# Seven block products for eight in the widening product of a decoder MLP (fp32 split in two halves), one core

## The chip, the core and the metric

One core of a Trainium2 chip runs the whole program. The metric is device time in microseconds (us), the median over runs. Engines: TensorE (PE; PEld is its weight load), VectorE (DVE), ScalarE (ACT), GpSimd (POOL), SyncE (SP, which issues most DMAs). Each engine works through its own queue in order.

## The reference, cut to what matters

Two layers over 576 tokens (512 of a prompt and 64 of a sample), model width 1024, MLP width 4096. Only the MLP at the end of a layer is touched by the change:

```python
    x = x + mixed @ w_o
    h2 = rmsnorm(x, norm2)
    x = x + jnp.square(jax.nn.relu(h2 @ w_up)) @ w_down
```

## The kernel before

Activations lie with features on the partitions: a tile of 128 features x 576 tokens. Every fp32 operand of a large product is cut into a high part (rounded to fp32r by a ScalarE cast) and a low part (what is left, by a VectorE subtraction). A product of two such operands is three matmuls: high x high, high x low, low x high. `gemm` (L222) makes one output tile: 8 k-tiles x 3 x 2 token ranges (256 and 320 columns, `HALF`), 48 matmuls, in one of two PSUM tiles (`mm`, two banks each).

Weights come as a list `seq` of 128 x 1024 tiles. `wfetch` (L106) issues their DMA on SP into `raw` (two slots), `wsplit` (L114) puts the ScalarE cast into `wh` (three slots) and notes the VectorE subtraction into `wl`, `settle` (L128) issues the noted subtractions. `wnext` (L132) is called where a weight tile is first used: there the cast of the tile two places ahead is put into ScalarE's queue, and its subtraction follows 1.2 us later by the planner's clock. The cast cannot run before TensorE has finished with the tile one place back, whose slot it takes.

The order of all queues is written by a planner: `tick` (L160) adds the estimated time of matmuls just issued to a clock `now`, and runs every generator in `sides` whose due time has come; a generator yields the delay to its next step. `post` puts a function there, `until` ticks until an event is due.

Around the change, in the layer loop:

- The product with w_o: eight output tiles f. `pair8` (L239) makes the first two, interleaved. Each is added to the residual `xs[f]` (VectorE), multiplied by the gain and split into `h2[f]`, then squared on ScalarE; GpSimd adds the squares into `sqs` (VectorE for f = 7).
- `stats` (L283), due 2.4 us after the last of these by the planner: TensorE sums `sqs` over features (`st`), VectorE and ScalarE form the reciprocal root (`rs`, with a ScalarE Sqrt), five VectorE products (`dg`), and TensorE spreads the result (`rps`) which ScalarE copies to `rb`.
- The widening product: chunks c of eight output tiles. For each, `gemm8` and then the generator `relu2`: VectorE takes max with 0 times `rb` (`z`), ScalarE squares (`zz`) and casts, VectorE subtracts, and one step of `movers` follows: a VectorE 1x1 copy (`beat`), a GpSimd 1x1 copy (`pace`) and a GpSimd DMA of a piece of the cache (`out_s`).
- The narrowing product `down` of chunk c - 1 follows the widening product of chunk c; in the last layer `last` takes the place of the last `down`.

Of the kernel before, what the change touches and what calls it, by code (L numbers as in the profile page):

```python
# [31 lines left out]
NCONST = _n  # L32

UNITS = ("d", "a", "b", "e", "c")


@with_exitstack
def hybrid_decoder_kernel(ctx: ExitStack, tc: tile.TileContext, a, o):
# [36 lines left out]
    def g2(l, k):  # L75
        return gains[:, 16 + 8 * l + k:16 + 8 * l + k + 1]
# [10 lines left out]
    for l in range(L):  # L87
        for p in range(2):
            for u, unit in enumerate(UNITS):
                if unit == "e" and p == 1:  # L90
                    continue
                seq += [(a["wq"][l, p, u, i], 1024) for i in range(2)]
        seq += [(a["wu"][l, g], 1024) for g in (3, 2, 1, 0)]
        for wg, wp_, m, lead in (("wgb", "wpb", 512, LEADB), ("wga", "wpa", 256, LEADA)):
            for f in range(8):
                seq += [(a[wg][l, i], 1024) for i in range(lead[f - 1] if f else 0, lead[f])]
                seq.append((a[wp_][l, f], m))
        seq += [(a["wo"][l, f], 1024) for f in range(8)]
        for c in range(5):
            if c < 4:  # L100
                seq += [(a["wup"][l, 8 * c + f], 1024) for f in range(8)]
            if c:
                seq += [(a["wd"][l, c - 1, f], 1024) for f in range(8)]
    raws, cut, owed, spare = [], [], [], []
    pos = [0, 0, 0]

    def wfetch(n):
        while pos[0] < min(n, len(seq)):
            src, w = seq[pos[0]]
            raw = wp.tile([128, 1024], F32, tag="raw", name="raw", bufs=2)  # L110
            Q.dma_start(raw[:, :w], src)
            raws.append((raw, w))
            pos[0] += 1

    def wsplit(n):
        while pos[1] < min(n, len(seq)):
            raw, w = raws[pos[1]]
            if pos[1] < len(seq) - 5:
                hi = wp.tile([128, 1024], F32R, tag="wh", name="wh", bufs=3)
                lo = wp.tile([128, 1024], F32R, tag="wl", name="wl", bufs=3)  # L120
            else:
                hi, lo = (spare.pop(0)().rearrange("p i n -> p (i n)") for _ in range(2))
            S.copy(hi[:, :w], raw[:, :w])
            owed.append((lo[:, :w], raw[:, :w], hi[:, :w].bitcast(F32)))
            cut.append((hi, lo))
            pos[1] += 1

    def settle():  # L128
        while owed:
            V.tensor_sub(*owed.pop(0))  # L130

    def wnext():  # L132
        i = pos[2]
# [102 lines left out]
    def gemm8(w, acts):  # L236
        return gemm([(*wcols(w, k), acts[k]) for k in range(8)])

    def pair8(acts):  # L239
        ws = wnext(), cut[pos[2]]  # L240
        tiles = [mmp.tile([128, 1024], F32, tag="mm", name="mm") for _ in range(2)]
        for n, ks in ((0, range(7)), (1, range(4)), (0, range(7, 8)), (1, range(4, 8))):
            for k in ks:
                for j, (m, x) in enumerate(((0, 0), (0, 1), (1, 0))):
                    for t0, t1, c0 in HALF:
                        T.matmul(tiles[n][:, c0:c0 + t1 - t0], wcols(ws[n], k)[m], acts[k][:, x, t0:t1],  # L246
                                 start=(k == 0 and j == 0), stop=(k == 7 and j == 2))
                tick(0.72)
        return [ps[:, 256:832] for ps in tiles]
# [106 lines left out]
    for l in range(L):  # L356
# [667 lines left out]
        for f in range(8):  # L1024
            pg = gates(LEADA, f)
            if f == 0:
                until("D", 1)
                dec_stack.close()
                mp_ = ms.enter_context(tc.tile_pool(name=f"mix{l}", bufs=8, side="right"))
            wa = wnext()  # L1030
            if pg is not None:
                gated(pg)
            ps = gemm([(*wcols(wa, k), oa[k]) for k in range(2)])
            t = gate.pop(0)
            V.scalar_tensor_tensor(out=t, in0=t, scalar=1.0, in1=ps, op0=ALU.add, op1=ALU.mult)
            (V if f == 7 else G).tensor_add(t, t, mB[f])
            m = mp_.tile([128, 2, NT], F32R, tag="m", name="m")
            split(m, t, 0.5)
            mixed.append(m)
# [5 lines left out]
        for k in range(NK):  # L1045
            xs.append(fp.tile([128, NT], F32, tag="x", name="xr"))
            post(2.1 + 0.8 * k, lambda k=k: Q.dma_start(xs[k], a["x"][k] if l == 0 else x_dr[k]))
        h2 = []
        sqs = tp.tile([128, NT], F32, tag="sqs", name="sqs", bufs=1)
        for f in range(8):  # L1050
            if f == 0:
                first = pair8(mixed)
            elif f == 1:
                wnext()
            ps = first.pop(0) if f < 2 else gemm8(wnext(), mixed)
            V.tensor_add(xs[f], xs[f], ps)
            t = fp.tile([128, 2, NT], F32R, tag="h2", name="h2")
            split(t, xs[f], g2(l, f))
            square(xs[f], sqs, f)
            h2.append(t)  # L1060
        side(stats(sqs, False, ("b", l)), 2.4)
        mark("ffn", l, lat=8.0)
        movers.append(copies(l))
        move(None)
        if l + 1 < L:
            sqs = tp.tile([128, NT], F32, tag="sqs", name="sqs", bufs=1)
        hn = []

        def down(c, fts):
            for f in range(8):  # L1070
                ps = gemm8(wnext(), fts)
                V.tensor_add(xs[f], xs[f], ps)
                if c == 3:
                    square(xs[f], sqs, f)
                    t = ap.tile([128, 2, NT], F32R, tag="a", name="a")
                    split(t, xs[f], g1(l + 1, f))
                    hn.append(t)
                    Q.dma_start(x_dr[f], xs[f])
                move(xs[f][0:1, 0:1])

        def relu2(c, ps, fts):
            t = fp.tile([128, NT], F32, tag="z", name="z", bufs=3)
            V.scalar_tensor_tensor(out=t, in0=ps, scalar=0.0, in1=scale_of["b", l][1], op0=ALU.max, op1=ALU.mult)
            t2 = fp.tile([128, NT], F32, tag="zz", name="zz", bufs=3)
            S.activation(t2, t, AF.Square)
            if c % 2 == 0:
                ft = ap.tile([128, 2, NT], F32R, tag="a", name="a")
            else:
                ft = mp_.tile([128, 2, NT], F32R, tag="m", name="m")
            split(ft, t2)  # L1090
            fts.append(ft)
            move(ft[0:1, 0, 0:1].bitcast(F32))
            return
            yield

        pend = None
        for c in range(4):
            fts = []
            for f in range(8):
                if f == 2:  # L1100
                    until("R", ("b", l))
                ps = gemm8(wnext(), h2)
                side(relu2(c, ps, fts), ("R", ("b", l)))
                tick()
            if pend is not None:
                down(c - 1, pend)
            pend = fts

        def finish(t0, t1, parts, end):
            n = t1 - t0  # L1110
# [32 lines left out]
                    yield 0.9  # L1143

        def last(fts):
            ws = []
            for t0, t1 in ((0, 320), (320, NT)):
                n = t1 - t0
                sq = tp.tile([128, NT], F32, tag="sqs", name="sqs", bufs=1)
                for f in range(8):  # L1150
                    if t0 == 0:
                        ws.append(wnext())
                    ps = mmp.tile([128, 1024], F32, tag="mm", name="mm")
                    for k in range(8):
                        for j, (w, x) in enumerate(((0, 0), (0, 1), (1, 0))):
                            T.matmul(ps[:, 0:n], wcols(ws[f], k)[w], fts[k][:, x, t0:t1],  # L1156
                                     start=(k == 0 and j == 0), stop=(k == 7 and j == 2))
                        tick(0.72 * n / NT)
                    x = xs[f][:, t0:t1]
                    V.tensor_add(x, x, ps[:, 0:n])  # L1160
                    t = sq if f == 0 else tp.tile([128, NT], F32, tag="t", name="sq")
                    S.activation(t[:, 0:n], x, AF.Square)
                    if 0 < f < 7:
                        G.tensor_add(sq[:, 0:n], sq[:, 0:n], t[:, 0:n])
                    S.activation(x, x, AF.Copy, scale=gf(f))
                    move(xs[f][0:1, t0:t0 + 1])
                side(finish(t0, t1, (sq, t), t0 > 0), 2.4 if t0 == 0 else 0.0)
            while sides:
                tick(0.3)

        if l + 1 < L:
            down(3, pend)
        else:
            spare += 8 * [lambda: fp.tile([128, 2, NT], F32R, tag="h2", name="h2")]
            spare += 2 * [lambda: ap.tile([128, 2, NT], F32R, tag="a", name="a")]
            last(pend)
        while movers:
            move(xs[7][0:1, 0:1])
        h = hn
# [127 lines left out]
```

## Time and profile before

| | us |
|---|---|
| median of three runs | 1769.35 (1768.34 to 1778.38) |
| the profiled execution | 1771.32 |
| its span, first to last instruction | 1769.3 |
| PE busy in the span | 1678.0 (95%) |
| DVE, ACT, POOL busy | 941.1, 553.6, 440.1 |
| mean granted TensorE clock | 0.971 |

A row of the groups view reads: line, engine, operation, out<-in by the program's tile names, shape, count | busy us, mean ns of one | idle time of the engine before them and who ended it. A row of the timeline reads: start us, duration us, engine, line, operation, tiles, shape, count [idle before <- who ended it]. L203 is the helper through which all VectorE, ScalarE and GpSimd operations go.

### The profile page before, as it was taken

What the parts mean: (1) busy time and instruction counts of PE and PEld (TensorE: products, weight loads), DVE (VectorE), ACT (ScalarE), POOL (GpSimd) and SP (SyncE); (2) the same over time, 40 slices, a digit from 0 to 9 for tenths busy, and PEclk for the clock granted to TensorE, in tenths of its full rate; (3) what the DMA queues carried; (4) which work ended last, traced back from release to release, by engine and by line L of the source; (5) the groups of instructions that cost most, each with busy time, mean ns of one, the idle gap of its engine ahead of it and who ended that gap; (6) DMA issues with size and microseconds to landing.
All of it is one profiled execution on the core that took longest, in us unless ns stands there. A gap on an engine that the chain in (4) does not pass through costs nothing. (4 is left out here: it accounts for less than half of the span.)

```text
span 1769.3 us, 30870 instructions
## 1 busy us (share of the span) xinstructions
PE 1678.0 (95%) x12992; PEld 1632.7 (92%) x12992; DVE 941.1 (53%) x1365; ACT 553.6 (31%) x882; POOL 440.1 (25%) x461
## 2 busy tenths in 40 slices
PE   8978799999999999999997897989999999999996
PEld 7978789989999999999997886888999999999996
DVE  6488679735444333343536975894454443433332
ACT  5523332223333222231334242311334331313232
POOL 2074129211111211110103712562111112121211
PEclk9979899999999999999999998999999999999998
DMA  5552654434254445443327336435243454444421
GB/s 171 170 163 66 219 158 127 135 105 155 85 186 165 171 155 178 153 170 109 130 74 229 118 116 208 136 100 163 78 157 120 169 168 166 167 166 164 165 84 54
DMA packets 140003, 255.22 MB, mean 144 GB/s; under 512 B 9660, under 2 KB 100284, under 8 KB 137034
## 3 DMA queue, kind: packets, MB, share of 16 engines
q1 hardware_dynamic: 135498, 198.46, 35.0%
q0 software_dynamic: 3648, 53.98, 8.6%
q8 instruction: 102, 1.67, 0.4%
q10 hardware_dynamic: 720, 0.82, 0.1%
q14 instruction: 35, 0.29, 0.1%
HBM read 239.40 MB, written 74.87 MB: 178 GB/s over the span
## 5 line engine op out<-in xcount | busy, mean ns | idle before, releaser
L228 PE MATMUL mm<-a,wh 128*128 128x256 f32 (+1 forms) x2304 | 413.2, 302 | 8.8 <-DVE tb L203 8.8
L203 DVE TENSOR_TENSOR wl<-raw,wh 128x1024 fp32r<-128x1024 f32 (+2 forms) x248 | 330.6, 1334 | 110.1 <-ACT wh L203 100.3
L203 ACT CAST wh<-raw 128x1024 fp32r<-128x1024 f32 (+2 forms) x248 | 241.4, 973 | 399.9 <-PE mm L228 301.4
L228 PEld LDWEIGHTS mm<-a,wh 128*128 128x128 f32 x2304 | 350.1, 192 | 16.9 <-issue 16.0
L228 PE MATMUL mm<-h,wh 128*128 128x256 f32 (+1 forms) x2048 | 354.8, 295 | 0.0
L228 PEld LDWEIGHTS mm<-h,wh 128*128 128x128 f32 x2048 | 306.2, 188 | 0.2
L203 POOL TENSOR_TENSOR prod<-kc,qb 128x1024 f32<-128x1024 f32 (+1 forms) x96 | 210.0, 2217 | 226.6 <-DMA kc<-in_c 183.8
L228 PE MATMUL mm<-a,wl 128*128 128x256 f32 (+1 forms) x1152 | 249.9, 299 | 0.0
L458 PE MATMUL mmq<-wh,a 128*128 128x256 f32 x1152 | 225.1, 295 | 3.2 <-DVE a L203 3.0
L228 PE MATMUL mm<-h,wl 128*128 128x256 f32 (+1 forms) x1024 | 218.1, 295 | 0.0
L203 POOL COPY pace<-beat 1x1 f32<-1x1 f32 x112 | 66.9, 597 | 545.1 <-DVE beat L203 545.1
L228 PE MATMUL mm<-m,wh 128*128 128x256 f32 (+1 forms) x1152 | 200.1, 295 | 0.0
L228 PEld LDWEIGHTS mm<-a,wl 128*128 128x128 f32 x1152 | 197.3, 192 | 0.0
L458 PEld LDWEIGHTS mmq<-wh,a 128*128 128x128 f32 x1152 | 187.4, 199 | 6.9 <-DVE a L203 3.8
L203 DVE TENSOR_TENSOR xr<-xr,mm 128x576 f32<-128x576 f32 (+2 forms) x88 | 61.5, 699 | 245.3 <-PE mm L228 223.1
L228 PEld LDWEIGHTS mm<-m,wh 128*128 128x128 f32 x1152 | 173.3, 187 | 0.0
L228 PEld LDWEIGHTS mm<-h,wl 128*128 128x128 f32 x1024 | 171.5, 188 | 0.0
L458 PE MATMUL mmq<-wl,a 128*128 128x256 f32 x576 | 167.4, 291 | 0.0
L203 ACT ACTIVATE zz<-z 128x576 f32<-128x576 f32 x64 | 43.9, 686 | 259.7 <-DVE z L203 259.7
L228 PE MATMUL mm<-m,wl 128*128 128x256 f32 x576 | 123.3, 295 | 0.0
L203 DVE SCALAR_TENSOR_TENSOR z<-mm,rb 128x576 f32<-128x576 f32 x64 | 48.5, 757 | 134.6 <-PE mm L228 128.1
L458 PEld LDWEIGHTS mmq<-wl,a 128*128 128x128 f32 x576 | 114.6, 199 | 0.0
(211 smaller groups left out, 1928.2 us busy)
## 6 DMA issues: line engine op xcount, KB each, us to landing
raw<-in_wup SPq DMA_DIRECT2D x64, 512.0 KB
raw<-in_wd SPq DMA_DIRECT2D x64, 512.0 KB
out_s<-in_c POOLq DMA_DIRECT2D x64, 508.0 KB, 4.0
kc<-in_c SPq DMA_DIRECT2D x40, 512.0 KB
raw<-in_wq SPq DMA_DIRECT2D x35, 512.0 KB
kc<-in_c SPq DMA_DIRECT2D x64, 256.0 KB
out_s<-in_c POOLq DMA_DIRECT2D x32, 504.0 KB, 4.7
raw<-in_wgb SPq DMA_DIRECT2D x16, 512.0 KB
```

The lines of the kernel that those rows point to most:

```text
L203: return op(*args, **kw)
L228: T.matmul(ps[:, c0:c0 + t1 - t0], w, act[:, x, t0:t1], start=(i == 0 and j == 0), stop=(i == n - 1 and j == 2))
L458: T.matmul(psm[:, j], x, ww, start=(k == 0 and i == 0 and j % 2 == 0), stop=(k == 7 and i == 2 and j % 2 == 1), skip_group_check=True)
```

## The change

One level of a seven-product (Strassen) scheme for h2 @ w_up. The tokens are cut in two halves of 288 (`NH`), the 1024 input features in two halves of four k-tiles, and two output tiles form a pair j (16 pairs). A pair takes seven products of four k-tiles x 3 matmuls of 288 columns, 84 matmuls in all, in place of 96 matmuls of 256 and 320 columns.

- Activations: `blocks(f)` replaces the split of `h2[f]` in the w_o stage and makes the operands B11, T1 (from f < 4) and B21, B22, T3, T2, T4 (from f >= 4 with xs[f - 4]), each split in high and low by `operand`.
- Weights: class `Two` fetches both tiles of a pair (`raw`, `raw1`). GpSimd forms two combinations in `first` (into `ws`) and, after the subtraction of the first weight tile, two in `second` (into r0 itself). A pair has four entries in the weight list, of 1024, 1024, 1024 and 512 columns, in place of two of 1024.
- `up(j)`: the product A accumulates through B11, T2, T3, T4 in one PSUM bank; ScalarE copies it out after B11 (`e1`) and T2 (`u2`) while it still grows, and after T4. T1 and B22 go to a bank `pc` (one slot) with a ScalarE copy `e5` between, B21 to a third. Three VectorE additions join them into the two tiles `z`, and `relu2` works on these.
- Chunks are of 5, 4, 4 and 3 pairs (`UPS`), each followed by the `down` of the same chunk. The last `down` and `last` begin with six k-tiles of two output tiles (`LATE`). `mp_` gets ten slots.

```diff
+    def first(self, eng):
+        h0, h1 = slice(0, 512), slice(512, 1024)
+        eng.tensor_add(self.s[:, h1], self.r1[:, h0], self.r1[:, h1])
+        eng.tensor_sub(self.s[:, h0], self.s[:, h1], self.r0[:, h0])
+
+    def second(self, eng):
+        h0, h1 = slice(0, 512), slice(512, 1024)
+        eng.tensor_sub(self.r0[:, h0], self.r1[:, h0], self.r0[:, h0])
+        eng.tensor_sub(self.r0[:, h1], self.r0[:, h1], self.s[:, h0])
...
+            two, w = seq[pos[1]]
+            then = None
+            if not isinstance(two, Two):
+                raw, w = raws[pos[1]]
+            elif w == 0:
+                raw, w = two.r0, 1024
+                two.s = fp.tile([128, 1024], F32, tag="ws", name="ws", bufs=2)
+                two.first(G)
+                then = two.second
+            else:
+                raw, w = ((two.s, 1024), (two.r0, 1024), (two.r1[:, 512:1024], 512))[w - 1]
...
         while owed:
-            V.tensor_sub(*owed.pop(0))
+            then, *args = owed.pop(0)
+            V.tensor_sub(*args)
+            if then is not None:
+                then(G)
...
+        def operand(pool, tag, bufs, src, names):
+            n = len(names)
+            t = pool.tile([128, 2, n * NH], F32R, tag=tag, name="h2", bufs=bufs)
+            S.copy(t[:, 0], src)
+            V.tensor_sub(t[:, 1], src, t[:, 0].bitcast(F32))
+            for i, name in enumerate(names):
+                ops[name].append(t[:, :, NH * i:NH * i + NH])
+
+        def blocks(f):
+            x = fp.tile([128, NT], F32, tag="z", name="z", bufs=3)
+            if f < 4:
+                S.activation(x[:, :NH], xs[f][:, :NH], AF.Copy, scale=g2(l, f))
+                V.scalar_tensor_tensor(out=x[:, NH:], in0=xs[f][:, NH:], scalar=g2(l, f), in1=x[:, :NH],
+                                       op0=ALU.mult, op1=ALU.subtract)
+                operand(ap, "a", 10, x, ("B11", "T1"))
+                return
+            S.activation(x, xs[f], AF.Copy, scale=g2(l, f))
+            operand(ap, "a", 10, x, ("B21", "B22"))
+            t = fp.tile([128, 3 * NH], F32, tag="e", name="e", bufs=1)
+            k = f - 4
+            V.scalar_tensor_tensor(out=t[:, :NH], in0=xs[k][:, NH:], scalar=g2(l, k), in1=x[:, NH:],
+                                   op0=ALU.mult, op1=ALU.subtract)
+            V.scalar_tensor_tensor(out=t[:, NH:NT], in0=xs[k][:, :NH], scalar=g2(l, k), in1=t[:, :NH],
+                                   op0=ALU.mult, op1=ALU.subtract)
+            V.tensor_sub(t[:, NT:], x[:, :NH], t[:, NH:NT])
+            operand(*((ap, "a", 10) if k < 2 else (fp, "h3", 2)), t[:, :NT], ("T3", "T2"))
+            operand(fp, "h4", 4, t[:, NT:], ("T4",))
...
-            t = fp.tile([128, 2, NT], F32R, tag="h2", name="h2")
-            split(t, xs[f], g2(l, f))
+            blocks(f)
             square(xs[f], sqs, f)
...
+        def relu2(z):
+            V.scalar_tensor_tensor(out=z, in0=z, scalar=0.0, in1=scale_of["b", l][1], op0=ALU.max, op1=ALU.mult)
+            yield 0.8
+            S.activation(z, z, AF.Square)
+            ft = mp_.tile([128, 2, NT], F32R, tag="m", name="m")
+            S.copy(ft[:, 0], z)
+            yield 1.5
+            V.tensor_sub(ft[:, 1], z, ft[:, 0].bitcast(F32))
             fts.append(ft)
             move(ft[0:1, 0, 0:1].bitcast(F32))
...
+            w = wnext()
+            product(A, w, 0, "B11", True, False)
+            S.copy(e1, A)
+            if j == 0:
+                w1 = wnext()
+                product(C_, w1, 1, "T1", True, False)
+                S.copy(e5, C_)
+            product(B, w, 1, "B21", True, True)
+            z_open()
+            V.tensor_add(z[0][:, :NH], e1, B)
+            if j:
+                w1 = wnext()
+            product(A, w1, 0, "T2", False, False)
+            S.copy(u2, A)
+            if j:
+                product(C_, w1, 1, "T1", True, False)
+                S.copy(e5, C_)
+            w = wnext()
+            product(A, w, 0, "T3", False, False)
+            z_open()
+            V.tensor_add(z[1][:, NH:], e5, A)
+            product(C_, w, 1, "B22", False, True)
+            V.tensor_add(z[0][:, NH:], u2, C_)
+            side(relu2(z[0]), ("R", ("b", l)))
+            w = wnext()
+            product(A, w, 0, "T4", False, True)
+            S.copy(z[1][:, :NH], A)
+            side(relu2(z[1]), ("R", ("b", l)))
+            tick()
```

## Rows read from the trace of the kernel before

**Rows 1.** The page: busy time of each engine over the span.
```profile
PE 1678.0 (95%) x12992; PEld 1632.7 (92%) x12992; DVE 941.1 (53%) x1365; ACT 553.6 (31%) x882; POOL 440.1 (25%) x461
```

**Rows 2.** Windows: a stretch of the second MLP (us; busy PE PEld DVE ACT POOL; PEclk; DMA; GB/s).
```profile
1400.00:1690.00 290.00, 290.00 (x2185) 290.00 (x2184) 112.32 (x163) 78.42 (x94) 49.71 (x96) 1.00 0.47 162
```

**Rows 3.** Timeline of VectorE: outputs of the widening product, second layer.
```profile
1354.62 0.76 DVE L203 SCALAR_TENSOR_TENSOR z<-mm,rb 128x576 f32<-128x576 f32 x1 [1.22 <-PE mm L228]
...
1360.97 0.76 DVE L203 SCALAR_TENSOR_TENSOR z<-mm,rb 128x576 f32<-128x576 f32 x1 [1.95 <-PE mm L228]
```

**Rows 4.** Timeline of VectorE in `last`: outputs of 24 matmuls of 320, then 256 columns.
```profile
1723.47 0.49 DVE L203 TENSOR_TENSOR xr<-xr,mm 128x320 f32<-128x320 f32 x1 [2.04 <-PE mm L1156]
1726.99 0.49 DVE L203 TENSOR_TENSOR xr<-xr,mm 128x320 f32<-128x320 f32 x1 [3.03 <-PE mm L1156]
...
1743.38 0.42 DVE L203 TENSOR_TENSOR xr<-xr,mm 128x256 f32<-128x256 f32 x1 [1.50 <-PE mm L1156]
1746.10 0.42 DVE L203 TENSOR_TENSOR xr<-xr,mm 128x256 f32<-128x256 f32 x1 [2.30 <-PE mm L1156]
```

**Rows 5.** Groups by form, 1360 to 1690 us: the MLP's VectorE and ScalarE operations.
```profile
L203 DVE TENSOR_TENSOR wl<-raw,wh 128x1024 fp32r<-128x1024 f32 x52 | 64.3, 1237 | 4.4 <-ACT wh L203 0.2
L203 ACT CAST wh<-raw 128x1024 fp32r<-128x1024 f32 x52 | 54.5, 1048 | 110.6 <-PE mm L228 110.6
...
L203 ACT ACTIVATE zz<-z 128x576 f32<-128x576 f32 x30 | 20.6, 686 | 125.0 <-DVE z L203 125.0
...
L203 DVE TENSOR_TENSOR m<-zz,m 128x576 fp32r<-128x576 f32 x16 | 12.1, 758 | 23.3 <-ACT m L203 23.3
L203 ACT CAST m<-zz 128x576 fp32r<-128x576 f32 x16 | 10.8, 673 | 0.5
```

**Rows 6.** Groups by form, whole span: GpSimd's 512-column operation and ScalarE's cast.
```profile
L203 POOL TENSOR_TENSOR prod<-kc,qb 128x512 f32<-128x512 f32 x32 | 41.5, 1318 | 22.9 <-DVE SC L203 12.3 <-DMA kc<-in_c 10.6
...
L203 ACT CAST wh<-raw 128x512 fp32r<-128x512 f32 x18 | 11.1, 615 | 39.5 <-PE mm L228 25.3 <-DMA raw<-in_wpb 12.1 <-DMA raw<-in_wq 2.1
```

**Rows 7.** Timeline: a ScalarE copy out of PSUM, near the end.
```profile
1756.21 0.37 ACT L203 COPY rb<-fb 128x256 f32<-128x256 f32 x1 [2.25 <-PE fb L1128]
```

**Rows 8.** Timeline, product with w_o: a VectorE subtraction issued during a GpSimd addition.
```profile
1315.69 1.44 POOL L203 TENSOR_TENSOR sqs<-sqs,sq 128x576 f32<-128x576 f32 x1 [4.96 <-ACT sq L203]
...
1316.52 1.69 DVE L203 TENSOR_TENSOR wl<-raw,wh 128x1024 fp32r<-128x1024 f32 x1 [0.69 <-ACT wh L203]
```

**Rows 9.** Timeline: VectorE additions from PSUM during a GpSimd addition.
```profile
1735.06 0.74 POOL L203 TENSOR_TENSOR sqs<-sqs,sq 128x256 f32<-128x256 f32 x1 [9.52 <-ACT sq L203]
...
1735.23 1.28 DVE L203 TENSOR_TENSOR xr<-xr,fb 128x320 f32<-128x320 f32 x3 [0.75 <-PE fb L1128]
```

**Rows 10.** Timeline: VectorE and ScalarE at the last w_o tile and the statistics.
```profile
1339.01 0.75 DVE L203 TENSOR_TENSOR xr<-xr,mm 128x576 f32<-128x576 f32 x1 [1.60 <-PE mm L228]
1340.61 0.82 DVE L203 SCALAR_TENSOR_TENSOR h<-xr,gains,h 128x576 fp32r<-128x576 f32 x1 [0.85 <-ACT h L203]
...
1339.80 0.78 ACT L203 ACTIVATE h<-xr,gains 128x576 fp32r<-128x576 f32 x1 [4.11 <-DVE xr L203]
...
1342.11 1.28 ACT L203 ACT_TABLE_LOAD   x1
...
1344.93 1.03 DVE L203 TENSOR_SCALAR dg<-const,rs 128x128 f32<-128x128 f32 x5
```

**Rows 11.** The chain of work that ended last, around the statistics (start, us, what).
```profile
1342.15 1.05 PE st L287 x8
...
1347.58 0.89 PE rps L308 x8
```

**Rows 12.** Windows around a TensorE stop of 8.9 us in the second layer's attention.
```profile
1070.00:1078.00 8.00, 0.00 (x0) 0.00 (x0) 1.70 (x5) 1.19 (x2) 0.88 (x5) 0.74 0.91 313
1078.00:1086.00 8.00, 6.29 (x26) 6.02 (x27) 5.05 (x14) 0.22 (x1) 6.05 (x10) 0.50 0.25 77
```

**Rows 13.** DMA issues: a cache piece, KB each, median us to landing.
```profile
out_s<-in_c POOLq DMA_DIRECT2D x64, 508.0 KB, 4.0
```

## What the change will do to the time

> **What bounds the kernel now.** I read the page first: PE is busy for 95% of the span, DVE for 53% [rows 1]. Then the windows of the MLP: TensorE has no gap in 290 us and full clock, DVE is busy for 39%, ACT for 27%, POOL for 17% [rows 2]. In this stage every matmul saved is time saved, as long as the other engines keep up. So the question is whether they do once a pair of outputs needs fewer matmuls and more of everything else. For that I read the timelines of the single engines for durations, hand-over times and for what two engines do to each other.
>
> **What is removed.** Outputs of the widening product follow each other by 6.35 us [rows 3], 48 matmuls; a pair takes 12.70. Alone, 24 matmuls of 320 columns take 3.52 us and of 256 columns 2.72 [rows 4], 0.147 and 0.113 each; halfway, a matmul of 288 is an estimated 0.131. A product of 12 is then 1.57, seven are 11.0. If TensorE stayed the bound, 32 pairs would give back 32 x 1.7 = 54 us.
>
> The Trainium skill (TensorE: Matmul & The Clock Gate, Back-to-back issue gap) gives N / 2.4 + 2.5 ns, 122.5 ns for 288 columns. By it 256 and 320 would be 109 and 136; the trace has 113 and 147 and decides. By the page's figure the sum below would be some 10 us lower (24 matmuls in each of 24 cycles, 84 in the other pairs).
>
> **What is added to a pair, by engine.** ACT: casts of 3 x 1024 and 512 columns for two of 1024, and four copies of 288 out of PSUM, estimated at 0.40 from 0.37 for 256 [rows 7]. DVE: subtractions likewise (1.24 for 1024, 0.70 estimated for 512), three additions from PSUM of 0.45 (0.42 and 0.49 for 256 and 320, [rows 4]). POOL: four operations of 512 columns, 1.3 each [rows 6]; before, only the mover's copy and DMA issue. Sums: ACT 7.9, DVE 9.2, POOL 5.2 and movers, against 11.0 of TensorE. None is over, but they are chained, and two of them meet at a port.
>
> **VectorE and GpSimd exclude each other.** In the w_o stage GpSimd adds from 1315.69 to 1317.13. A VectorE subtraction of 1024 columns that is issued at 1316.52 takes 1.69 instead of 1.24 and ends at 1318.21, 1.08 after GpSimd: about its streaming time alone [rows 8, 5]. So a VectorE operation with two SBUF inputs waits until GpSimd's operation is over. VectorE additions with one input in PSUM are not held: three of 320 columns, the first of them begun in the middle of a GpSimd addition, take 1.28 together, less than three times 0.49 [rows 9, 4].
>
> **The steady pair.** I walk the queues from the end of T1 (t = 0). Hand-overs: 0.04 from one engine to another (1339.76 to 1339.80 in [rows 10]); from the start of TensorE's next product to a reader of the last one's bank 0.2, an estimate, since a matmul's end lies behind the next one's start.
> ACT copies e5 to 0.60, casts the next pair's first weights to 1.60; DVE subtracts to 2.87. That stands ahead of the addition that frees bank A (T3 ended at 1.57, addition to 3.28), so T4 starts at 3.38, 0.24 late. GpSimd's `second` starts at 2.93: first half to 4.23. B22 ended at 3.14; z0's addition ends at 3.79, but relu2's max (two SBUF inputs) waits for the port: 4.23 to 4.85. GpSimd's second half then holds it to 6.15, and the subtraction of the next weight tile, behind, runs to 7.22. ACT meanwhile: square z0 to 5.57, cast to 6.27, copy out T4 to 6.58, weight cast. Then z1's max on DVE 7.15 to 7.90, ACT square to 8.62, cast to 9.32, and only then the copy e1 of the next pair, long since computed (B11): to 9.63. T2 accumulates onto that bank and starts at 9.73; T2 and T1 take 3.14. The cycle is 12.87, of which TensorE runs 11.0. Durations: [rows 5, 6, 7]. The port waits make 0.8 of it: without them it is 12.1. GpSimd's `first` fits behind the movers while DVE waits for e5. The first pair of a chunk has no z1 ahead of it: 11.0 + 0.2. At chunk ends `LATE` gives 12 k-tiles, 9.5 us, for tails of some 5.7: nothing. The weight loads keep number and size; both of a pair are issued about 16 us ahead of their cast, against 4.0 to landing for a piece of that size [rows 13], on SP, which nothing new blocks: nothing. Movers issue as many pieces as before, later on POOL; nobody waits for them.
>
> **The opening of the stage.** For f >= 4 `blocks` makes ACT and DVE hand over to and fro: residual 0.75, scaled copy 0.78, high part 0.67, low part 0.76 (end 3.07); two scaled differences (0.52 each, estimate: 0.82 less 288 columns' streaming) and one plain (0.46) end at 4.55; high and low of T3/T2 end at 5.57, of T4 at 5.94 [rows 5, 10]. Then comes the square (5.72), GpSimd's addition (5.76 to 7.2), the next weight cast (to 6.7) and its subtraction, which waits for GpSimd: 8.27. The next residual stands behind it: 8.2 us a tile against TensorE's 6.35. So f = 7 begins 3 x 1.8 = 5.5 late. `first` and `second` of pair 0 fall into f = 6 and 7 too and hold the port for 5.2 us, of which I count 2.5 as delay (0 to 5). The last residual is then at 8.2 after TensorE ends w_o, the last low part at 14.1, `sqs`, which comes last now, at 14.9; before, the statistics could begin 3.1 after that residual did [rows 10, 11]. The statistics' matmuls stand in TensorE's queue after B11 and half of T1. TensorE waits there until S0 = 15.0.
> From S0: statistics 1.05 [rows 11], rest of T1 0.79, B21 1.57: 3.41. The cast of the pair's last weights waits for B21 and stands before the Sqrt: 4.2, table load 5.5, to the end of `dg` 2.57 more as before [rows 10]: 8.1; rps 9.0 [rows 11], rest of T2 9.8, copy u2 and hand-overs 10.5 (pair 0 has T3 straight behind), three products: 15.2. Pair 0 ends 30.2 after w_o. Before, two outputs ended at 1354.42 and w_o at 1338.81, taken 0.2 ahead of the rows: 15.6 [rows 3, 10]. After TensorE stood still from 1070 to 1078, rows show a clock of 0.50, 1.2 GHz of 2.4, for 8 us with 6.3 us of matmuls [rows 12], which costs half of these. Here about 5 us run behind a longer stop: 2.5 (0 to 3.1).
>
> **Sum for a layer.** Before: 15.6 + 30 x 6.35 = 206.1. After: pair 0 with clock 32.7, three first pairs 33.6, twelve others 154.4: 220.7. Two layers: +29. The profiled execution took 1771.3, 2.0 over the median of the runs; 1800.5 there is 1798 for the median. A difference under 1% (18 us) is about what a measurement of this kernel can't tell from no change.
>
> **Rivals.**
> - The port does not decide (VectorE gets its turns between GpSimd's operations). Cycle 12.1; opening tiles 7.9, S0 11.4, pair 0 29.1 with clock. 207.9 a layer: 1773. For it: GpSimd works for only 5.2 of 12.9 us. Against: [rows 8].
> - The port costs more: VectorE's queued subtraction goes ahead of GpSimd's waiting half, or `first` slips behind a mover and delays the subtraction before T4. Each moves the cycle by 0.4; both give 13.7 and 24 x 0.85 = 20 more: 1818. The Trainium skill (SBUF — State Buffer, Terms) says that of the two engines the loser of the shared port fully blocks, for the full instruction; read so that it holds for additions from PSUM too, z0's addition would wait as well, a cycle longer by 1.1, 1825. The trace does not bear this reading out: [rows 9].
> - On the other side: the place of e1's copy in ACT's queue. If it stood ahead of z1's square and cast (due 0.8 us after T4, half of B11 by the planner), T2 would start after the weight cast, the cycle would be 11.2, and 24 x 1.67 = 40 come off: 1758, faster. By a cycle of 11.6 the whole is even. Against: B11's copy is issued 1.6 after T4 by the planner, and ACT takes its queue in order.
> - Fewer matmuls do not make shorter products (a floor for each, at 0.132): only +1 to 3, contained in the range.
>
> **How the numbers follow.** Forecast 0.52, port does not decide 0.20, port costs more 0.13, e1 ahead 0.15. The forecast's own range is 1783 to 1809 (port in the opening 0 to 5 and clock 0 to 3.1, twice, and 0.2 either way on the cycle). The whole: 1760 to 1820, which leaves out the lower half of the last rival (with an opening shorter as well) and the upper part of the third. Slower by over 1% (above 1787): most of the forecast and the third, 0.60. Within: part of the forecast, the second, half of the last, 0.27. Faster: 0.13.
>
> **What would show it.** In the profile after: 384 matmuls fewer, 12 a pair; TensorE stops of about 1.9 us before T2, once a pair, ended by ACT's e1; VectorE's `wl` and `z` lengthened where GpSimd's `ws` or `raw` runs; one stop of over 10 us at each `st`, ended by `sqs`, with a clock of 0.5 behind it. Wrong it would be if the pairs follow each other by 11 to 11.5 us, or if `sqs` is ready within 5 us of the last residual.

## The result: slower by 8.5%, where 1.6% was forecast

| | before | after |
|---|---|---|
| median, four runs each | 1772.23 | 1922.69 (1919.32 to 1927.09) |
| ratio, 95% interval | | 1.0847 [1.0804, 1.0890] |
| profiled execution | 1771.32 | 1921.10 |
| forecast | | 1798 (1760 to 1820) |

The direction was right; the size was not: +150 us against the +29 that the prediction's sum adds to the kernel before. The page of the profile after, its span and its busy times (compare [rows 1]):

```profile
span 1919.3 us, 30712 instructions
PE 1705.4 (89%) x12608; PEld 1637.6 (85%) x12608; DVE 1106.3 (58%) x1573; ACT 668.7 (35%) x1106; POOL 629.0 (33%) x589
```

The 384 matmuls are gone (12992 to 12608) and yet TensorE is busy for longer, 1705.4 against 1678.0: some of them run at a lower clock (mean granted clock 0.934, before 0.971). Its idle time went from about 91 us to 214. The view of waits says for whom (engine, tile and line waited for: us in total, times, longest; L1167 is the matmul in `product`, L244 the planner's helper by which ScalarE, VectorE and GpSimd are issued; PEld is the weight load ahead of the same matmul):

```profile
PEld mm L1167 <- ACT e L244: 79.7, 32, 3.1
PE mm L1167 <- ACT e L244: 71.9, 32, 2.9
PEld mm L1167 <- DVE z L244: 37.2, 32, 4.8
PE mm L1167 <- DVE z L244: 27.4, 32, 4.5
```

Two stops in each of the 32 pairs, where I had forecast one. The timeline shows which product stops (start, duration, engine, line, operation; in brackets the idle time before it and what ended it):

```profile
1603.77 0.29 PE L1167 MATMUL mm<-h,wl 128*128 128x288 f32 x1
1603.87 1.05 ACT L244 CAST wh<-raw 128x1024 fp32r<-128x1024 f32 x1
...
1605.19 0.68 ACT L244 ACTIVATE z<-z 128x576 f32<-128x576 f32 x1 [0.28 <-DVE z L244]
1605.91 0.67 ACT L244 CAST m<-z 128x576 fp32r<-128x576 f32 x1
...
1606.48 0.39 ACT L244 COPY e<-mm 128x288 f32<-128x288 f32 x1
...
1606.93 0.85 PE L1167 MATMUL mm<-h,wh 128*128 128x288 f32 x2 [2.87 <-ACT e L244]
...
1610.23 1.28 POOL L244 TENSOR_TENSOR ws<-ws,raw 128x512 f32<-128x512 f32 x1
1610.29 0.45 DVE L244 TENSOR_TENSOR z<-e,mm 128x288 f32<-128x288 f32 x1 [2.54 <-PE mm L1167]
...
1610.80 0.53 PE L1167 MATMUL mm<-h,wh 128*128 128x288 f32 x2 [0.61 <-DVE z L244]
```

B11 ends near 1604. ScalarE has its result copied only at 1606.87 (`e`), behind the weight cast, z1's square and its cast: that queue order is the one of the prediction. But the product that waits for the copy is the very next one, B21, which writes the other bank. T2 then starts at 1610.80, not after `e1` but after VectorE's addition of `e1` and B, which reads that other bank and which T2 doesn't need at all. The chain of waits has the same step, with the duration of the whole product (start, us, engine, tile, line, matmuls), and the windows have the clock (us; busy PE PEld DVE ACT POOL; PEclk; DMA; GB/s):

```profile
1606.93 3.26 PE mm L1167 x12
...
1614.26 1.59 PE mm L1167 x12
```

```profile
1602.30:1606.90 4.60, 1.76 (x14) 1.52 (x12) 4.60 (x5) 4.24 (x7) 1.10 (x1) 1.00 0.00 0
1607.00:1611.00 4.00, 3.38 (x13) 3.04 (x14) 1.46 (x5) 0.62 (x1) 3.81 (x6) 0.59 0.88 269
```

Behind the stop of 2.87 us B21 takes 3.26: TensorE ran at 1.2 GHz of 2.4 for most of it. In the pair before it, behind a stop of the same length, the clock stayed at 1.00 and B21 took 1.86 (timeline, chain of waits, windows):

```profile
1591.63 0.53 PE L1167 MATMUL mm<-h,wh 128*128 128x288 f32 x2 [2.86 <-ACT e L244]
```

```profile
1591.63 1.86 PE mm L1167 x12
```

```profile
1591.50:1595.50 4.00, 3.25 (x22) 3.02 (x23) 2.78 (x6) 0.69 (x2) 3.61 (x6) 1.00 0.80 259
```

The pair around 1607 takes 16.7, by the additions that take in B22:

```profile
1600.77 0.45 DVE L244 TENSOR_TENSOR z<-e,pc 128x288 f32<-128x288 f32 x1 [0.21 <-PE pc L1167]
1617.48 0.45 DVE L244 TENSOR_TENSOR z<-e,pc 128x288 f32<-128x288 f32 x1 [0.21 <-PE pc L1167]
```

Over the 24 pairs inside chunks (all but the first of each chunk) it is 14.9 to 18.0, 16.9 on average. In 22 of them the stops are the same 2.9 and 0.6; what differs is how long the lower clock lasts.

By stages: +76 in the first layer's MLP, +68 from the end of the second layer's w_o to the end of the program (498.3 against 430.5), 6 elsewhere.

### The profile page after: what moved, and what is told of

Same layout as the page of the kernel before. It is cut to its first block, busy times and chain, and to the rows that moved or that the text cites. A ratio compares the mean times of both kernels' runs of the same rounds, so it can differ in the third digit from the quotient of the medians.

```text
span 1919.3 us, 30712 instructions
## 1 busy us (share of the span) xinstructions
PE 1705.4 (89%) x12608; PEld 1637.6 (85%) x12608; DVE 1106.3 (58%) x1573; ACT 668.7 (35%) x1106; POOL 629.0 (33%) x589
## 3 DMA queue, kind: packets, MB, share of 16 engines
q1 hardware_dynamic: 135498, 198.46, 31.7%
## 5 line engine op out<-in xcount | busy, mean ns | idle before, releaser
L244 DVE TENSOR_TENSOR wl<-raw,wh 128x1024 fp32r<-128x1024 f32 (+2 forms) x280 | 372.6, 1332 | 248.1 <-ACT wh L244 247.4
L244 ACT CAST wh<-raw 128x1024 fp32r<-128x1024 f32 (+2 forms) x280 | 261.4, 934 | 468.9 <-PE mm L269 280.0
L1167 PE MATMUL mm<-h,wh 128*128 128x288 f32 x1280 | 302.3, 330 | 99.4 <-ACT e L244 71.9
L269 PE MATMUL mm<-m,wh 128*128 128x256 f32 x2112 | 366.8, 295 | 0.0
L1167 PEld LDWEIGHTS mm<-h,wh 128*128 128x128 f32 x1280 | 230.7, 212 | 120.2 <-ACT e L244 79.7
L269 PEld LDWEIGHTS mm<-m,wh 128*128 128x128 f32 x2112 | 317.6, 187 | 0.0
L244 POOL TENSOR_TENSOR prod<-kc,qb 128x1024 f32<-128x1024 f32 (+1 forms) x96 | 208.3, 2195 | 231.2 <-DMA kc<-in_c 103.5
L269 PE MATMUL mm<-a,wh 128*128 128x256 f32 (+1 forms) x1280 | 238.0, 310 | 12.3 <-DVE mB L244 7.9
L269 PE MATMUL mm<-m,wl 128*128 128x256 f32 (+1 forms) x1056 | 225.9, 295 | 0.0
L269 PEld LDWEIGHTS mm<-a,wh 128*128 128x128 f32 x1280 | 198.6, 197 | 20.1 <-issue 19.5
L1167 PE MATMUL mm<-h,wl 128*128 128x288 f32 x640 | 207.1, 324 | 0.0
L244 POOL COPY pace<-beat 1x1 f32<-1x1 f32 x112 | 75.0, 670 | 358.7 <-DVE beat L244 358.7
L244 DVE TENSOR_TENSOR xr<-xr,mm 128x576 f32<-128x576 f32 (+2 forms) x88 | 61.4, 697 | 221.5 <-PE mm L269 194.7
L269 PEld LDWEIGHTS mm<-m,wl 128*128 128x128 f32 x1056 | 176.9, 187 | 0.0
L269 PE MATMUL mm<-a,wl 128*128 128x256 f32 (+1 forms) x640 | 140.9, 303 | 0.0
L1167 PEld LDWEIGHTS mm<-h,wl 128*128 128x128 f32 x640 | 137.4, 215 | 0.0
L1167 PE MATMUL pc<-h,wh 128*128 128x288 f32 x512 | 111.7, 311 | 8.9 <-ACT wh L244 8.9
```

The source lines that it names most:

```text
L244: return op(*args, **kw)
L269: T.matmul(ps[:, c0:c0 + t1 - t0], w, act[:, x, t0:t1], start=(i == 0 and j == 0), stop=(i == n - 1 and j == 2))
L1167: T.matmul(dst, w[m][:, c], ops[name][k][:, x], start=(start and k == 0 and j == 0), stop=(stop and k == 3 and j == 2), skip_group_check=True)
```

## The experiments

In the code A is bank 0 and B is bank 1 of one PSUM tile `ps` of 1024 columns. **Theory 1**: waits are kept for the tile, not for the bank, so whoever writes into one bank waits for the last reader of either. Every pair is then a chain: B11, copy e1, B21, addition to z0, T2. The rivals: GpSimd's combinations at the port are the main cost, or the place of e1's copy is, as in the prediction. The first four kernels, and `e5_bank_ahead` and `e7_bank_open` later, each ran once; beside the first four ran one of the kernel before (1768.89).

A layer's widening stage is taken here as in the prediction's sum: from its first product to its last, without the `down` between. Outside the two stages the profiled runs differ among themselves, by up to 8.5 us before the first stage (465.8 to 474.3) and by up to 8 between the two (503.7 to 511.8). Where a single run differs by no more than that, the stages say more than the time.

**B in a tile of its own** (`e1_bank`).

```diff
-            A, B, C_ = ps[:, 0:NH], ps[:, 512:512 + NH], pc[:, 0:NH]
+            pb = pdp.tile([128, 512], F32, tag="d", name="pbank")
+            A, B, C_ = ps[:, 0:NH], pb[:, 0:NH], pc[:, 0:NH]
```

> B21 gets a PSUM bank of its own (the idle bank of tag d) and so a tile of its own; nothing else changes. Theory 1: in the changed kernel A and B21 are two banks of one PSUM tile, and every product into the tile waits for the last reader of either bank, so B21 waits for ScalarE's copy of e1 and T2 for VectorE's z0 addition, 32 times each, and TensorE's clock falls behind the longer stops. Then the stop moves to T2, B21 runs under the chain, the pairs follow each other by 12.9 us (my walk) instead of 16.7, and the time is 1810 to 1835. Theory 2: the late copy e1 is the whole cause and the shared tile only names the place: T2 takes over all of the stop, only the 0.6 us ahead of T2 goes, pairs by 15.5 to 16, time 1890 to 1905.

Measured 1797.39, 125 us less by this one edit: 13 below theory 1's range, whose pairs of 12.9 came out, and far from theory 2's. Its waits and two of the additions of B22:

```profile
PE mm L1167 <- ACT e L244: 33.5, 26, 2.5
...
1506.68 0.45 DVE L244 TENSOR_TENSOR z<-e,pc 128x288 f32<-128x288 f32 x1 [0.21 <-PE pc L1167]
...
1512.84 0.53 PE L1167 MATMUL mm<-h,wh 128*128 128x288 f32 x2 [1.29 <-ACT e L244]
...
1519.52 0.46 DVE L244 TENSOR_TENSOR z<-e,pc 128x288 f32<-128x288 f32 x1 [0.21 <-PE pc L1167]
```

VectorE's `z` has gone from the waits, the stop stands before T2, and a pair takes 12.84. The clock between 1494 and 1532 is 1.00, stops of 1.29 included. Theory 1 holds for both stops.

**The copy of e1 first, the tile left shared** (`e2_ahead`): z1's square is due 1.7 us after T4 instead of 0.8, and so stands behind the next pair's copy in ScalarE's queue.

```diff
-        def relu2(z):
+        def relu2(z, due=0.8):
...
-            yield 0.8
+            yield due
...
-            side(relu2(z[1]), ("R", ("b", l)))
+            side(relu2(z[1], 1.7), ("R", ("b", l)))
```

> Only the order of ScalarE's queue changes: the square and the cast of a pair's second output come 0.9 us later by the planner, behind the next pair's copy e1 instead of ahead of it; A and B21 still share a tile. Theory 1 (shared tile, e1 at the end of ScalarE's chain): e1 comes 1.6 us sooner, the stop before B21 shrinks from 2.9 to about 1.3, half-clock products go, pairs by 13.7 to 14.5, time 1850 to 1870. Theory 3 (VectorE and GpSimd excluding each other at the port is what is short): ScalarE's order changes nothing that lasts, time within 10 us of 1921.

Measured 1840.35: 82 us less than the change, and 10 below the lower edge of what was expected. Pairs take 13.6 where 13.7 to 14.5 were expected: the stops before B21 are down to 1.2 and cost no clock (1.00 from 1528 to 1555). The copy's place matters as long as B21 waits for it; the wait for VectorE stays, 27.5 us in 32 stops. Neither this nor `e1_bank` alone is the whole.

**GpSimd's four combinations left out**, with the tile shared (`e3_nocomb`) and with B apart (`e4_bank_nocomb`).

```diff
-                two.s = fp.tile([128, 1024], F32, tag="ws", name="ws", bufs=2)
-                two.first(G)
-                then = two.second
+                two.s = two.r1
```

> GpSimd's four combinations of weights are left out (the second tile itself takes the place of the sum, the first tile stays as it was), so that the products are of other numbers; every cast, subtraction, matmul and wait on a load stays. Theory 3 (the port): VectorE's z and wl lose their extra 0.2 and 1.1 us, and most of the loss goes, time 1790 to 1830. Theory 1 (shared tile): only 0.6 to 1 us a pair goes, as ScalarE's chain is still ahead of B21, time 1885 to 1905.

> Both: B21 in a bank and tile of its own, and GpSimd's combinations left out (the products are of other numbers). Theory 1 with my walk: without the waits at the port the cycle is 12.1 instead of 12.9, and the opening of each layer ends some 3 us sooner; 1785 to 1805, some 25 below the kernel with the bank alone. Theory 3: the port is most of it and the bank adds little: within 10 us of the kernel without combinations alone.

Measured 1913.62 and 1771.59. The port is not what made the change slow: taking these combinations away gives back 9 of 150, less than theory 1 expected and far from the rival's 1790 to 1830. With B apart the same step gives 25.8 (22 of it in the two stages), as expected and as the prediction's sum has it for the port (1798 less 1773), though the time itself lies 13 below its range.

Why only 9 with the tile shared? The waits and the busy time of `e3_nocomb` say it (compare 71.9 and 1705.4 above; its line 1165 is L1167 of the others, L242 their L244):

```profile
PE mm L1165 <- ACT e L242: 58.6, 32, 2.5
```

```profile
PE 1712.3 (90%) x12608; PEld 1645.0 (86%) x12608; DVE 1066.5 (56%) x1573; ACT 666.4 (35%) x1106; POOL 442.3 (23%) x461
```

The stop before B21 does get shorter, 2.25 instead of 2.87 in a steady pair, by the same 0.6 as the stop before T2 between `e1_bank` and `e4_bank_nocomb` (1.29 to 0.69). But TensorE is busy for 7 us longer with the same matmuls. Behind 20 such stops in each kernel the clock falls, and B21, T2 and T1, 5.1 together at full clock, take 7.6 on average here against 7.1 in the kernel after. The lower clock takes most of the gain back.

The next three add to `e1_bank` what the prediction names as late. The kernel before had 1773.39 over that call.

**e1 first, B apart** (`e5_bank_ahead`, both edits).

> B21 in a bank and tile of its own, and the second output's square and cast behind the next pair's copy e1 in ScalarE's queue. My walk with ScalarE's order as the last link: TensorE no longer stops before T2, but pairs do not reach 11.2 us, as GpSimd's first half of the combinations then slips behind the second mover into VectorE's subtraction ahead of T4: 11.7 to 12.2 for 12.8, time 1765 to 1778. If the port does not matter: 11.2, 1759. If the order does not matter once the bank is apart: 1797.

Measured 1789.19: 8 less instead of 20 to 30; in the two stages alone it is 15. Only the second pair of a chunk takes 11.3 to 11.4, and not in the last chunk; the others take 12.7 to 12.9, as before. The timeline:

```profile
1500.06 2.16 POOL L244 TENSOR_TENSOR ws<-ws,raw 128x512 f32<-128x512 f32 x1
...
1502.26 1.05 ACT L244 CAST wh<-ws 128x1024 fp32r<-128x1024 f32 x1 [2.58 <-POOL ws L244]
...
1506.26 1.04 ACT L244 CAST wh<-raw 128x1024 fp32r<-128x1024 f32 x1 [1.36 <-POOL raw L244]
1507.21 0.39 ACT L244 COPY e<-mm 128x288 f32<-128x288 f32 x1
```

With z1's end later, the mover's copies and with them GpSimd's `first` come later, `first` meets VectorE's subtraction (2.16 instead of 1.30), and the weight casts, which now wait for GpSimd, hold up the copy of e1 that stands behind them. A stall moved, from ScalarE's queue to GpSimd's.

**The opening shortened** (`e7_bank_open`): the square ahead of `blocks`, the three differences ahead of the split of B21/B22, and pair 0's second weight tile taken without putting the next cast into the queue.

```diff
+            square(xs[f], sqs, f)
             blocks(f)
-            square(xs[f], sqs, f)
...
             if j == 0:
-                w1 = wnext()
+                w1 = cut[pos[2]]
...
-            if j:
-                w1 = wnext()
+            w1 = wnext()
```

> B21 in a tile of its own, and only the opening of the stage changed: the square and its sum come ahead of the making of the operands, the three differences are made before the first low part is waited for, and the cast of pair 0's last weights comes behind B21 in the program, so that the Sqrt does not stand behind it. My walk: the statistics' matmuls wait 10 instead of 14.5 us after w_o, and what follows them is some 4 shorter: pair 0 ends 22 to 25 after w_o instead of 31.7, time 1780 to 1785. If TensorE's wait for the statistics is covered by another wait (operands or weights of pair 0): over 1790.

Measured 1791.35, 6 less than `e1_bank` and just inside the second case, whose condition holds in part: in the second layer the stop before the statistics falls from 5.28 to 0.92, while the stops for pair 0's weights stay (4.3, and 1.7 instead of 0.8). The statistics start 10.8 after w_o instead of 14.5, and pair 0 ends after 25.4 instead of 30.3 (second layer; in the first 25.4 instead of 29.9). The 31.7 of the expectation takes in the next pair's first product, so part of the gain that it forecasts was never there. The stages are shorter by 5.9 and 3.3 us. Of these 9, 3 are gone between the two stages, where the runs differ by more than that anyway.

**All of it, and the weight casts later** (`e8_all`: a cast two places ahead is put into the queue 1.7 us later, a subtraction likewise), and the same with all four combinations on VectorE (`e9_all_onV`: `first(V)`, `then(V)`).

> The two before together, and two orders more: the cast of the tile two places ahead comes behind e1 too, and the subtraction of the next pair's first weights behind the addition that frees bank A. If the two engines at the port are the last bound, VectorE and GpSimd need some 11.3 to 12 us a pair there: time 1750 to 1765. If TensorE becomes the bound (11.1 a pair): 1740.

> As the one before, and the four combinations of weights on VectorE instead of GpSimd: about 0.6 us each there against 1.3 of excluded time. The port theory: VectorE's own work rises to some 10.5 of 11.1 us, but nothing excludes it: 1735 to 1755, below the one before. If VectorE's queue in order is what binds: pairs of 12 us or more, above the one before.

Measured 1798.39 (ratio 1.0133 [1.0088, 1.0178]) and 1775.28 (1.0014 [0.9997, 1.0030]): both expectations were too low by 20 us or more, and `e9_all_onV` has the long pairs of its second case and yet lies below `e8_all`. In `e8_all` the middle pairs of a chunk take 14.0; all four of GpSimd's operations now run in a row against VectorE's:

```profile
1506.81 2.49 DVE L247 TENSOR_TENSOR wl<-raw,wh 128x1024 fp32r<-128x1024 f32 x1
1506.90 1.31 POOL L247 TENSOR_TENSOR ws<-raw 128x512 f32<-128x512 f32 x1
1508.28 2.17 POOL L247 TENSOR_TENSOR ws<-ws,raw 128x512 f32<-128x512 f32 x1
...
1510.49 1.05 ACT L247 CAST wh<-ws 128x1024 fp32r<-128x1024 f32 x1 [4.99 <-POOL ws L247]
```

Both sides pay: 2.49 for 1.24, 2.17 for 1.30. On VectorE the four give 23 us back, and then these pairs take 13.15, with VectorE's additions no longer waiting for TensorE. The last runs leave the later casts out (`e10_open_onV` is `e9_all_onV` without them: no difference). The kernel before had 1771.10 beside the next three.

**The combinations on VectorE, then on both** (`e6_bank_onV`: `e1_bank` with `first(V)` and `then(V)`; `e10_open_onV`: that with the opening and e1 first; `e11_open_split`: as the last, but only `first` on VectorE and `then(G)` kept).

> B21 has its own PSUM tile, as in e1_bank (1797), and the four weight combinations of a pair are done by VectorE instead of GpSimd; nothing is left out. If the 26 us between e1_bank and e4_bank_nocomb are what VectorE waits for GpSimd at their port, nearly all of them come back, less what four more operations of 512 columns (some 0.7 each, 2.8 a pair) cost in VectorE's own order: 1776 to 1788, pairs 12.2 to 12.6 apart. If they are the work itself and not the port, VectorE's longer queue costs as much as the waits did: 1795 or more, pairs 12.8 or more apart.

> Everything that gained by itself, without the late weight casts of e8_all and e9_all_onV: B21's own tile, the shorter opening (6 us in e7_bank_open), z1's square behind the copy of e1 (8 us in e5_bank_ahead), the combinations on VectorE. If these add up: e6_bank_onV less 14, that is 1762 to 1774, no slower than the kernel before. If VectorE's queue now sets the pair (in e9_all_onV 13.15), the gain of the earlier copy is given back: within 4 us of e9_all_onV's 1775 or above it.

> As e10_open_onV, but only the first two combinations on VectorE, the other two on GpSimd, where they run while VectorE has the additions out of PSUM. If half the port's price comes with half of GpSimd's operations and VectorE's queue has room: within 5 us of e10_open_onV, above it by up to 13 if the port binds (1775 to 1787); if VectorE's own queue binds, it is below e10_open_onV by 3 to 10 us.

Measured 1807.50 (1.0211 [1.0189, 1.0234]), 1775.59 (1.0027 [1.0013, 1.0041]) and **1749.21 (0.9885 [0.9865, 0.9905])**. The first falls clearly to its second case: moved to VectorE without anything else, the work costs some 10 us more than the port did. `e10_open_onV` falls to its second case too, while `e11_open_split` lies 26 below it, where its third case had 3 to 10. The place where it binds, in `e10_open_onV`:

```profile
1485.95 1.23 DVE L244 TENSOR_TENSOR wl<-raw,wh 128x1024 fp32r<-128x1024 f32 x1 [0.87 <-ACT wh L244]
1487.21 0.69 DVE L244 TENSOR_TENSOR raw<-raw,raw 128x512 f32<-128x512 f32 x1
1487.82 0.68 DVE L244 TENSOR_TENSOR raw<-raw,ws 128x512 f32<-128x512 f32 x1
1488.42 0.45 DVE L244 TENSOR_TENSOR z<-e,mm 128x288 f32<-128x288 f32 x1
...
1488.92 0.54 PE L1167 MATMUL mm<-h,wh 128*128 128x288 f32 x2 [1.21 <-DVE z L244]
```

`second`, 1.2 us of work that TensorE needs only later, stands in VectorE's queue ahead of the addition that frees bank A, and T4 is 1.21 late; over the span it is 26.7 us in 22 stops. With `second` back on GpSimd the addition follows the subtraction at once (windows of `e11_open_split`, columns as above, and its additions of B22):

```profile
1455.00:1490.00 35.00, 35.00 (x261) 34.55 (x261) 31.81 (x46) 23.51 (x37) 15.26 (x18) 1.00 0.45 151
```

```profile
1466.70 0.46 DVE L244 TENSOR_TENSOR z<-e,pc 128x288 f32<-128x288 f32 x1 [0.21 <-PE pc L1167]
1478.00 0.46 DVE L244 TENSOR_TENSOR z<-e,pc 128x288 f32<-128x288 f32 x1 [0.21 <-PE pc L1167]
```

TensorE has no gap: a pair takes 11.3, against 12.70 before [rows 3]. VectorE is at 91%. This kernel is faster than the change and than the kernel before, than the latter by 22 us or 1.2%. More doesn't come because the opening still costs: pair 0 ends 23.3 after w_o in the second layer (15.6 before), and the last pair of a layer takes 1.5 longer, so a layer is 23.3 + 15 x 11.3 + 1.5 = 194 against 206, 12 less, and 13 less in the first layer. All four combinations on GpSimd with this opening and order, but without the later casts, were not run.

**The shared tile alone** (`e12_split_onetile`: `e11_open_split` with the line of `e1_bank` taken back).

> e11_open_split with one thing undone: A and B are again two banks of one PSUM tile. What the shared tile costs by itself once nothing else is late. If it is two hand-overs a pair (B21 waits for the copy of e1, which starts 0.2 into the next product at best and takes 0.40; T2 waits for VectorE's addition of e1 and B, 0.45 and up to 0.9 behind another operation), TensorE stands about 1.5 to 2 us a pair, 32 pairs: 1797 to 1813 at full clock, 1815 to 1835 if the clock falls behind the stops. If the shared tile cost only what the late copy of e1 made of it, with the copy in time it costs under 0.3 a pair: below 1760.

Measured 1814.41 (1.0271 [1.0254, 1.0289]; the kernel before 1767.13 beside it, 4 less than beside `e11_open_split`), 65 us more than `e11_open_split`:

```profile
PE mm L1167 <- ACT e L244: 32.2, 33, 1.2
...
PE mm L1167 <- DVE z L244: 19.9, 32, 0.7
...
1503.94 0.54 PE L1167 MATMUL mm<-h,wh 128*128 128x288 f32 x2 [1.16 <-ACT e L244]
...
1506.41 0.53 PE L1167 MATMUL mm<-h,wh 128*128 128x288 f32 x2 [0.62 <-DVE z L244]
```

With every other delay mended, two hand-overs a pair remain, 1.16 and 0.62 here, at full clock (1.00 from 1486 to 1513). The result lies 1 us above the case expected for full clock. So the shared tile costs 65 us where nothing else is late and 125 where the copy of e1 is.

## Why the prediction was right in its direction and wrong in its size

**The step that failed** is in the walk of the steady pair. It lets B21 run under ScalarE's chain and holds up only T2: "T2 accumulates onto that bank and starts at 9.73". B21 does not run under the chain: it waits for the copy of e1, and T2 waits once more behind it. Put in what the runs showed and the same walk comes out: the copy of e1 lets B21 start at 9.73, B21 takes 3.26, hand-over and addition 0.61, T2 and T1 3.2: a cycle of 16.8, where 16.7 was measured in the pair shown and 12.87 forecast.

By the prediction's own terms, first and second layer where they differ (us; the pairs inside chunks as range and mean):

| | pair 0 | three first pairs, each | twelve pairs inside chunks | layer |
|---|---|---|---|---|
| forecast | 32.7 | 11.2 | 12.87 | 220.7 |
| the kernel after | 37.4, 35.8 | 12.9 | 14.9 to 18.0, 16.9 | 282.4, 273.8 |
| `e1_bank` | 29.9, 30.3 | 11.3 | 12.6 to 12.9 but for the last, 15.4 and 14.0 | 220.1, 219.1 |
| `e4_bank_nocomb` | 27.1, 28.1 | 11.3 | 12.2 to 12.5 | 208.0, 208.9 |

The profiled execution took 1921.1 against the 1800.5 that the prediction has for it, 121 more. The 24 pairs inside chunks make 96 of that, the two pairs 0 make 8, the six first pairs 10, and 6 lie outside the stages. In pair 0, T2 waits 4.5 and 4.4 for the addition to z0, behind VectorE's part of the statistics. Of the 4.0 that a pair inside a chunk takes beyond the forecast, some 2.4 are the waits (the two pairs that kept the full clock behind a stop of 2.9 take 15.3), and 1.6 is the mean price of the clock.

No row of before shows such a wait: there the two banks of a `mm` tile are read together, once both are done. But the change makes a tile whose banks are read and written in turns for the first time, and a new hand-over that no row shows has to be bounded from both sides like a new operation. I set this one at nothing without a sentence.

That the wait belongs to the program and not to the memory, `e11_open_split` shows: B21's product into `pbank` runs from 1469.85 to 1471.4, and ScalarE reads `mm` at 1470.70 for 0.40, its usual time. The Trainium skill (PSUM — Partial Sum Buffer, PSUM bank collisions raise a hardware error) asks that two engines be kept apart within one bank and the same 32 partitions, and says that accesses to different banks run clean; that agrees, and it means that neither of the two waits guarded the bank that the product writes.

**Right, by the runs with B apart, and in part by luck.** `e1_bank` is the kernel that I costed: 1797.39 against 1798, a layer 220.1 and 219.1 against 220.7, a pair 12.84 against 12.87, T2 ended by ACT's `e`, the opening's statistics 14.5 after w_o (15.0). The order in ScalarE's queue was as told. Under these sums some terms cancel. The stop before T2 was 1.29, where about 1.9 was forecast, and the products took 0.3 more than forecast. Pair 0 took 2.4 to 2.8 less than forecast: behind the statistics' stop the clock was at 0.51 for 8 us, and the slower products filled the time in which the walk has TensorE wait for the result of the statistics (it stood for 0.5 of the 15.8 us from there to the end of the pair). The last pair of a layer took 1.2 to 2.5 more. The one stop of over 10 us that the prediction names as a sign came as two: 4.47 before T1, ended by a weight cast, and 5.28 before the statistics, ended by `sqs`.

The cost of the port, 25.8 against 25, is shown by `e4_bank_nocomb`, whose layers are 208.0 and 208.9 against 207.9 in the prediction's first rival. That VectorE's additions out of PSUM are not held by it [rows 9] shows again in after: GpSimd works from 1610.23 for 1.28, and the addition at 1610.29 takes 0.45.

**Terms that were off.** A matmul of 288 columns takes 0.134 (11.28 for 84 in `e11_open_split`) where halfway between [rows 4] was 0.131. By the figure that the Trainium skill (TensorE: Matmul & The Clock Gate, Back-to-back issue gap) gives for an isolated matmul, 122.5 ns, seven products would take an estimated 10.3; here, as with [rows 4], the trace lies above it. The clock term stood in the opening alone; it belonged to most pairs. Pieces of the cache landed after 5.5 us instead of 4.0 [rows 13], and nobody waited for them.

**The rivals.** "The port does not decide" is refused by `e4_bank_nocomb`. "e1 ahead" had 40 us for the copy's place; with B apart it gave 8 (`e5_bank_ahead`; 15 in the stages), since the weight casts then wait for GpSimd: the rival's cycle of 11.2 assumed that nothing else comes late, and needs the split of `e11_open_split` as well. Its end of the scale was real: 1749, by mending four things, not one.

Left open: why the clock fell behind 20 of the 22 stops of 2.9 us and not behind the other two.

## What to carry to other kernels

When two results live in different banks, give them tiles of their own, or the program may make one wait for the other's readers; look in the trace for a matmul that waits for the reader of something it doesn't write. When an operation is moved to another engine, ask what stands behind it there: the same 512-column work cost least when half of it went to VectorE, where nothing urgent stood behind it, and half stayed on GpSimd. Ask of a stop also what the clock does behind it: here the waits added 2.4 us to a pair and the clock another 1.6.

## What the runs showed of the hardware

Inside the chunks, TensorE's stops of 1.29 us in `e1_bank` and of 1.16 and 0.62 in `e12_split_onetile` left the granted clock at 1.00. Behind 20 of the 22 stops of 2.9 in the kernel after it fell: it stood at 0.59 over the 4 us from 1607, and twelve matmuls took 3.26. Behind the other two it stayed at 1.00, and twelve took 1.86. In the last pair of `e1_bank`, behind a stop of 2.49 in either layer, it fell in the first (0.57 from 834 to 838) and not in the second (twelve matmuls in 1.87). So in these runs the length of a stop alone does not tell whether the clock falls. I had expected it only at the long stops of the opening ([rows 12] is a stop of 8.9).

GpSimd pays at the port too: the 512-column operation takes 1.30 alone, and 2.16 in `e5_bank_ahead` and 2.17 in `e8_all` where VectorE's subtraction goes first.
